# Moving the block turns and the loads of y to GpSimd's queue, lowering the rank of the square transposes, and pairing two output blocks of each down projection

## The chip, the cores and the metric

The kernel runs on one core of a Trainium2 chip. The metric is the device time of one execution in microseconds. The kernel before takes 2028.07 us (median of 3 runs, 2026.43 to 2028.74). The profile comes from one more execution, which took 2025.24 us.

## The reference, cut to what matters

One layer of a streaming encoder is computed for 384 rows: 256 prompt frames of one stream, and 16 new frames of each of 8 running streams. All data are float32.

```python
h    = rmsnorm(x, norm_mix_g)
proj = h @ w_in                                   # GLU halves, q, k, v, forget logits, gates A and B
u    = glu_in[..., :D_CONV] * sigmoid(glu_in[..., D_CONV:])
z    = layernorm(causal_dwconv(ext, conv_dw_w, conv_dw_b), conv_ln_g, conv_ln_b)
a_out = (z * sigmoid(z)) @ conv_pw_out
b_out = attn_fn(q, k, v, logf) @ w_att_out
x    = x + (gate_a * a_out + gate_b * b_out) @ w_out
h2   = rmsnorm(x, norm_ffn_g)
up   = h2 @ w_up                                  # gate half g and value half u, 5632 columns each
gc   = causal_dwconv(ext_f, ffn_dw_w, ffn_dw_b)   # 3 taps on the gate half
x    = x + (silu(gc) * u_half) @ w_down
```

`D_MODEL` is 2048, `D_FF` 5632. The change touches the last three products: `conv_pw_out`, `w_out`, and the up and down projections.

## The kernel before, in words

**Rows and splitting.** The 384 rows are three tiles of 128 (`NTT = 3`). Every product is made from split operands: each is kept as `hi`, a copy in the type fp32r, and `lo`, what the copy leaves over, and each product of two 128-row blocks takes three matmuls (L233 to L235): hi by hi, hi by lo, lo by hi. The activations are split once. The weights are streamed: `fetch` (L129, queue of SyncE) loads 512 KB, two contraction blocks of 128 by 512 columns, into one of three `raw` buffers. `split` makes `hi` on ScalarE (L138, two buffers) and `lo` on VectorE (L139, two buffers). One such chunk feeds 18 matmuls of 512 columns (2 contraction blocks, 3 row tiles, 3 matmuls).

**Jobs.** `gemm` takes a list of jobs. A job is one 512-column output block: `nk` contraction steps, three PSUM banks `acc` (one for each row tile; the pool has 5 banks), then `evac` for each bank and `done`. Jobs in a tuple share their steps: chunk by chunk the first job's two steps, then the second's; its third bank comes from the pool `misc`. Before the change only the first two jobs of v are paired. `plan` lists the weight chunks in the order in which jobs take them.

**Turning.** A product's output has rows on partitions, but the next product needs it with columns on partitions. The class `Turned` does this for blocks of 128 by 512 for each of three row tiles. First, `swap` transposes 32x32 squares on VectorE (L247). Second, `quadrants_out` (L253) writes the squares to DRAM with four DMAs of 192 KB (`turn<-block`). Third, `quadrants_in` (L259) reads them back in the turned order with one DMA of 768 KB (`block<-turn`), which waits for all four. There are 30 such turns: four in the `conv_pw_out` stage (`pw_job`, giving `mix`), four in the `w_out` stage (`wo_job`, giving `xg`), and 22 in the up projections (a gate half and a value half for each of 11 groups). One more, of the state of the FFN convolution (`sft`), is written out beside them.

**What follows a turn.** For `mix`, ScalarE copies the turned block to `hi` (L882) and VectorE makes `lo` (L883). For `xg`, it is L931 to L933. For a gate half, ScalarE copies into `extf` (L978), GpSimd fills the borders (L981 to L985), VectorE does the taps (L997, L999). For a value half, VectorE multiplies (L1013), ScalarE and VectorE split (L1017, L1018) into `act`. The FFN runs in the order of `FFN_PLAN`: up groups 0 to 4, down over groups 0 to 3, up 5 to 8, down over 4 to 7, up 9 and 10, down over 8 to 10. Each down projection has four jobs, one for each 512 output columns, and adds into `y` (L1039).

**Order.** TensorE's order is written out by hand. On the other engines a scheduler fixes one order for each engine when the program is built; an instruction with a higher rank goes first among those that it holds ready. The rank is the place in the program, moved forward inside `tc.high_priority(offset=...)`: 150 places for fetch and split, 60 for `evac`, 400 for the turn's DMAs. On the chip each engine and each DMA queue then keeps to that order: an instruction that waits holds up all behind it. All of the weight loads, turn DMAs and loads of `y` (L907) are in SyncE's queue.

**The two stages with most of the changed work.** In `pw_job`, `ev` does on VectorE, at the rank of `evac`, for each row tile: gate times bank (L872), add of the other branch (L873), and the swap (L247). In `wo_job` it is the add to `y` (L919) and the swap. In `up_jobs`, ScalarE moves the bank to `rows` (L1030), and VectorE swaps.

Of the kernel before, what the change touches and what calls it, by code (L numbers as in the profile page):

```python
# [11 lines left out]
ALU = mybir.AluOpType  # L12
# [3 lines left out]
P = 128  # L16
DM = 2048
NT = 384
NTT = 3
# [10 lines left out]
CONV_START = 56  # L30
CONV_RATE = ((CONV_START, 0.0), (176, 1.3), (240, 0.6), (1 << 20, 1.4))
LN_LAG = 4
SPLIT_AHEAD, EVAC_AHEAD, MOVE_AHEAD = 150, 60, 400

R_FFN, R_DWB, R_LNG, R_LNB, R_FDB, R_QG, R_N = 0, 16, 24, 32, 40, 84, 85
WARM, WARM_MID, WARM_END = 6, 2, 4
# [3 lines left out]
def hybrid_step(  # L40
# [9 lines left out]
    nc = tc.nc  # L50
# [23 lines left out]
    def f(ap):  # L74
        return ap.bitcast(F32)
# [3 lines left out]
    tt = nc.vector.tensor_tensor  # L79
# [6 lines left out]
    xin = [x_prompt[0, 0:P, :], x_prompt[0, P:2 * P, :], x_sample.rearrange("b t d -> (b t) d")]  # L86
# [57 lines left out]
    def planned(w, k0, cols, nk, *more):  # L144
        for k in range(k0, k0 + nk, 2):
            for cl in (cols,) + more:
                plan.append([w[0, k * P:(k + 2) * P, c:c + n].rearrange("(k p) n -> p k n", p=P) for c, n in cl])

    def up_cols(g):
        return [[(512 * g, 512)], [(DFF + 512 * g, 512)]]  # L150
# [7 lines left out]
    N_COLS = [[(512 * g, 512)] for g in range(4)]  # L158
# [13 lines left out]
    for what, g in FFN_PLAN:  # L172
        if what == "up":
            for cols in up_cols(g):
                planned(w_up, 0, cols, 16)
        else:
            for cols in N_COLS:
                planned(w_down, 4 * g[0], cols, 4 * len(g))

    v_last = len(plan) - 16  # L180
# [4 lines left out]
    def after(units, fn):  # L185
        later.append([units, fn])
# [8 lines left out]
    def grouped(tiles):  # L195
        def get(k):
            t = tiles[k // 4]
            return t[:, 0, k % 4, :], t[:, 1, k % 4, :]
        return get
# [46 lines left out]
    def swap_blocks(dst, src, q):  # L246
        nc.vector.transpose(dst.rearrange("p i q c -> p q i c"), src.rearrange("p (q i c) -> p q i c", q=q, i=4))  # L247

    def quadrants_out(src, n):
        d = p_dr.tile([4, 32, 4, n], F32, tag="turn", bufs=4, name="turn")  # L250
        with tc.high_priority(offset=MOVE_AHEAD):
            for i in range(4):
                nc.sync.dma_start(d[:, :, i, :].rearrange("j r n -> r j n"),  # L253
                                  src[32 * i:32 * i + 32, :].rearrange("r (j n) -> r j n", j=4))
        return d

    def quadrants_in(dst, d):
        with tc.high_priority(offset=MOVE_AHEAD):
            nc.sync.dma_start(dst, d[:].rearrange("j r i n -> (j r) (i n)"))  # L259

    class Turned:
        def __init__(self, block, rows):
# [1 line left out]
            w = self.work[:].rearrange("p (i t q c) -> p i t q c", i=4, t=NTT, c=32)  # L264
            self.w = [w[:, :, t] for t in range(NTT)]

        def swap(self, t):
            swap_blocks(self.w[t], self.rows[:, t, :], 4)

        def moved(self):  # L270
            out = self.block()
            quadrants_in(out[:], quadrants_out(self.work[:], 384))
            return out[:].rearrange("p (i t q c) -> p i t q c", i=4, t=NTT, q=4)

    def natural(ap):
        return ap.rearrange("p (t i c) -> p i t c", t=NTT, i=4)
# [5 lines left out]
    def job(kind, nk, act, evac, n=512, done=None):  # L282
        d = dict(kind=kind, nk=nk, act=act, evac=evac, n=n)
        if done is not None:
            d["done"] = done
        return d
# [61 lines left out]
    def panels(name):  # L348
        return [p_sg.tile([P, NTT, 512], F32, tag=f"S{n}", name=f"{name}{n}") for n in range(4)]
# [208 lines left out]
    def tiny(name):  # L558
        return p_qkv.tile([P, NTT, H], F32, name=name)

    z, e, r, s2, pl = tiny("lz"), tiny("le"), tiny("lr"), tiny("ls"), tiny("lpoly")
# [212 lines left out]
    sgA = panels("sgA")  # L774
# [20 lines left out]
    sgB = [p_z.tile([P, NTT, 512], F32, name=f"sgB{n}") for n in range(4)]  # L795
# [69 lines left out]
    def pw_job(g):  # L865
        box = []

        def ev(t, ps):
            if t == 0:
                box.append(Turned(mix_block, sgA[g]))  # L870
            a, b = sgA[g][:, t, :], sgB[g][:, t, :]
            tt(a, ps[:], a, op=ALU.mult)  # L872
            tt(a, a, b, op=ALU.add)  # L873
            box[0].swap(t)

        def done():
            d = box[0].moved()

            def parts(m):
                v = d[:, :, :, m, :]  # L880
                hi, lo = natural(mix[g][:, 0, m, :]), natural(mix[g][:, 1, m, :])
                nc.scalar.copy(hi, v)  # L882
                tt(lo, v, f(hi), op=ALU.subtract)  # L883
            for m in range(4):
                after(3 + m // 2, lambda m=m: parts(m))
        return job("B", 8, grouped(zt), ev, done=done)
# [14 lines left out]
    y = []  # L901

    def load_y():
        y.extend(panels("y"))
        for n in range(4):
            for t in range(NTT):
                nc.sync.dma_start(y[n][:, t, :], xin[t][:, n * 512:(n + 1) * 512])  # L907

    def block():
        return p_w.tile([P, NTT * 512], F32, tag="block", bufs=4, name="block")  # L910

    def wo_job(n):
        box = []

        def ev(t, ps):
            ys = y[n][:, t, :]
            if t == 0:
                box.append(Turned(block, y[n]))
            tt(ys, ps[:], ys, op=ALU.add)  # L919
            box[0].swap(t)  # L920
            jk = p_w.tile([P, 512], F32, tag="jk", bufs=1, name="jk2")
            nc.scalar.activation(jk[:], ys, AF.Square, accum_out=ss2[:, t, n:n + 1])

        def done():
            d = box[0].moved()

            def parts(m):
                v = d[:, :, :, m, :]
                g = col[:, R_FFN + 4 * n + m:R_FFN + 4 * n + m + 1]
                hi, lo = natural(xg[n][:, 0, m, :]), natural(xg[n][:, 1, m, :])  # L930
                nc.scalar.activation(v, v, AF.Identity, scale=g)  # L931
                nc.scalar.copy(hi, v)
                tt(lo, v, f(hi), op=ALU.subtract)  # L933
            for m in range(4):
                after(3 + m // 2, lambda m=m: parts(m))
            if n == 3:
                second_norm()
        return job("B", 16, grouped(mix), ev, done=done)

    def second_norm():  # L940
        m2 = p_w.tile([P, NTT], F32, name="m2")
        nc.vector.tensor_reduce(m2[:], ss2[:], axis=mybir.AxisListType.X, op=ALU.add)
        ts(m2[:], m2[:], 1.0 / DM, EPS, op0=ALU.mult, op1=ALU.add)
        newton_rsqrt(r2[:], p_w.tile([P, NTT], F32, name="r2s")[:], m2[:])

    after(8, load_y)
    gemm([wo_job(n) for n in range(4)])
    p_f, close_f = pool("ffn")
# [5 lines left out]
    for i in range(4):  # L954
        nc.sync.dma_start(sr[32 * i:32 * i + 16, :], sf_rows[:, 1408 * i:1408 * (i + 1)])
    swap_blocks(sw.rearrange("p (i q c) -> p i q c", i=4, c=32), sr, 11)
    quadrants_in(sft[:].rearrange("p a c -> p (a c)"), quadrants_out(sw, 352))

    extf = [p_f.tile([P, 24, 18], F32, name=f"extf{m}") for m in range(4)]
# [62 lines left out]
    def up_jobs(g):  # L1022
        def half(finish):
            box = []

            def ev(t, ps):
                if t == 0:
                    rows = block()[:].rearrange("p (t n) -> p t n", t=NTT)
                    box.append(Turned(block, rows))
                nc.scalar.activation(box[0].rows[:, t, :], ps[:], AF.Identity, scale=r2[:, t:t + 1])  # L1030
                box[0].swap(t)
            return job("B", 16, xa, ev, done=finish(g, box))
        return [half(up_g_done), half(up_u_done)]

    def down_jobs(gs, last):
        def evac(n):
            def ev(t, ps):
                ys = y[n][:, t, :]
                tt(ys, ps[:], ys, op=ALU.add)  # L1039
                if last:  # L1040
                    dst = [y_prompt[0, 0:P], y_prompt[0, P:2 * P], y_sample.rearrange("b t d -> (b t) d")][t]
                    nc.sync.dma_start(dst[:, n * 512:(n + 1) * 512], ys)
            return ev

        def act(k):
            return grouped([acts[g] for g in gs])(k)

        return [job("B", 4 * len(gs), act, evac(n)) for n in range(4)]

    for what, g in FFN_PLAN:  # L1050
        gemm(up_jobs(g) if what == "up" else down_jobs(g, g[-1] == 10))
# [45 lines left out]
```

## Time and profile before

| | |
|---|---|
| runs | 2028.07 us median (2026.43 to 2028.74) |
| profiled execution | 2025.24 us, of which 2023.5 us is the span from the first to the last instruction |
| granted TensorE clock over the span | 0.997 |
| VectorE busy | 1054.6 us (52%) |
| ScalarE busy | 772.5 us (38%) |
| GpSimd busy | 96.7 us (5%) |
| DMA | 324.63 MB, mean 160 GB/s; the queue of SyncE's DMAs 52.2% of 16 engines' span |

The page gives busy times, the busy share in 40 slices, the chain that ended last, and groups of instructions. In rows of the timeline the first number is the start in us from the beginning of the span, the second the length, then engine, line, operation and tiles; in brackets stands the engine's idle time just before and what ended it. An engine name with a q (SPq) is a queue's issue of a DMA, not the transfer. Matmuls overlap, so their starts, not their lengths, give the pace.

### The profile page before, as it was taken

Reading aid. Unit: us, or ns where it says so; the run is one execution under the profiler, and the core shown is the slowest. Engines: PE = TensorE matmul, PEld = TensorE weight load, DVE = VectorE, ACT = ScalarE, POOL = GpSimd, SP = SyncE. Lnnn points to the kernel's source line nnn. Section 1 sums busy time; section 2 is a strip of 40 time slices with the busy share of each in tenths; the row PEclk is TensorE's granted clock in tenths of the full one; section 3 lists DMA queues with packets and bytes.
Section 4 is the critical chain, followed back from the end, with each engine's and each line's share of the span. In section 5 each row is a group of like instructions: output and inputs, shape, how many; then the busy total and the mean of one; then the engine's idle time right before and its main releaser. Section 6 shows DMA issues by size and latency. Waiting matters only on the chain.

```text
span 2023.5 us, 24649 instructions
## 1 busy us (share of the span) xinstructions
PE 2004.1 (99%) x9498; PEld 1689.0 (83%) x9498; DVE 1054.6 (52%) x1459; ACT 772.5 (38%) x1148; POOL 96.7 (5%) x251
## 2 busy tenths in 40 slices
PE   9999999999999998999999999999999999999999
PEld 9999888888888886888888888888888888888877
DVE  4477868547466346454545545433445554334543
ACT  5433344555325332344434334222333332223422
POOL 1000100000000000000100111000100110001000
PEclk9999999999999999999999999999999999999999
DMA  6444645554344446756655565544555554446543
GB/s 187 133 133 113 201 144 167 171 161 141 115 127 125 127 144 194 243 168 190 198 178 179 176 189 160 163 132 128 172 183 172 177 182 138 133 126 193 166 162 125
DMA packets 197340, 324.63 MB, mean 160 GB/s; under 512 B 14542, under 2 KB 80585, under 8 KB 197215
## 3 DMA queue, kind: packets, MB, share of 16 engines
q1 hardware_dynamic: 196615, 322.35, 52.2%
q8 instruction: 74, 1.21, 0.3%
q0 software_dynamic: 288, 0.57, 0.2%
q14 instruction: 43, 0.35, 0.1%
q10 hardware_dynamic: 320, 0.14, 0.0%
HBM read 291.30 MB, written 32.17 MB: 160 GB/s over the span
## 4 chain that ended last, share of the span: by engine, by line
PE 97%; DVE 1%; DMA 1%; ACT 0%; issue 0%; SPq 0%; ACTq 0%; DVEq 0%
PE acc L234 29%; PE acc L233 29%; PE acc L235 29%; PE acc L230 2%; PE acc L228 2%; PE acc L229 2%; DVE lo L139 0%; DMA raw<-in_w_up_dram 0%; PE misc L673 0%; PE misc L299 0%; DVE sgA L872 0%; PE misc L739 0%; PE misc L706 0%; ACT hi L138 0%; DMA turn<-block 0%
## 5 line engine op out<-in xcount | busy, mean ns | idle before, releaser
L139 DVE TENSOR_TENSOR lo<-raw,hi 128x1024 fp32r<-128x1024 f32 (+2 forms) x481 | 579.4, 1205 | 842.0 <-ACT hi L138 837.6
L138 ACT CAST hi<-raw 128x1024 fp32r<-128x1024 f32 (+2 forms) x481 | 498.3, 1036 | 1080.1 <-PE acc L235 955.7
L234 PE MATMUL acc<-lo,xg 128*128 128x512 f32 x1056 | 410.9, 389 | 0.7 <-DVE lo L139 0.7
L233 PE MATMUL acc<-hi,xg 128*128 128x512 f32 x1056 | 410.8, 389 | 0.0
L235 PE MATMUL acc<-hi,xg 128*128 128x512 f32 x1056 | 410.8, 389 | 0.0
L233 PE MATMUL acc<-hi,hT 128*128 128x512 f32 (+1 forms) x704 | 272.1, 386 | 0.1
L234 PE MATMUL acc<-lo,hT 128*128 128x512 f32 (+1 forms) x704 | 265.7, 377 | 0.3 <-DVE lo L139 0.3
L235 PE MATMUL acc<-hi,hT 128*128 128x512 f32 (+1 forms) x704 | 265.7, 377 | 0.0
L234 PEld LDWEIGHTS acc<-lo,xg 128*128 128x128 f32 x1056 | 198.2, 188 | 42.3 <-DVE lo L139 1.1
L233 PEld LDWEIGHTS acc<-hi,xg 128*128 128x128 f32 x1056 | 198.2, 188 | 41.2
L235 PEld LDWEIGHTS acc<-hi,xg 128*128 128x128 f32 x1056 | 198.2, 188 | 41.0
L233 PE MATMUL acc<-hi,act 128*128 128x512 f32 x528 | 206.2, 391 | 3.4 <-ACT act L1017 3.4
L234 PE MATMUL acc<-lo,act 128*128 128x512 f32 x528 | 206.1, 390 | 0.0
L235 PE MATMUL acc<-hi,act 128*128 128x512 f32 x528 | 206.0, 390 | 0.0
L502 DVE SCALAR_TENSOR_TENSOR ut<-ext,cw,ut 128x384 f32<-128x384 f32 x240 | 150.0, 625 | 5.9
L233 PEld LDWEIGHTS acc<-hi,hT 128*128 128x128 f32 x704 | 132.2, 188 | 23.7 <-issue 1.8
L235 PEld LDWEIGHTS acc<-hi,hT 128*128 128x128 f32 x704 | 132.1, 188 | 23.3
L234 PEld LDWEIGHTS acc<-lo,hT 128*128 128x128 f32 x704 | 132.4, 188 | 22.3 <-DVE lo L139 1.6
L233 PEld LDWEIGHTS acc<-hi,act 128*128 128x128 f32 x528 | 99.4, 188 | 24.6 <-ACT act L1017 3.8
L235 PEld LDWEIGHTS acc<-hi,act 128*128 128x128 f32 x528 | 99.5, 188 | 20.9 <-DVE act L1018 0.3
L234 PEld LDWEIGHTS acc<-lo,act 128*128 128x128 f32 x528 | 99.5, 188 | 20.7
L228 PE MATMUL acc<-hT,hi 128*128 128x384 f32 x256 | 86.0, 336 | 0.1
(289 smaller groups left out, 1943.2 us busy)
## 6 DMA issues: line engine op xcount, KB each, us to landing
raw<-in_w_up_dram SPq DMA_DIRECT2D x176, 512.0 KB
raw<-in_w_in_dram SPq DMA_DIRECT2D x96, 512.0 KB
raw<-in_w_down_dram SPq DMA_DIRECT2D x88, 512.0 KB
turn<-block SPq DMA_DIRECT2D x120, 192.0 KB
block<-turn SPq DMA_DIRECT2D x30, 768.0 KB
raw<-in_w_in_dram SPq DMA_DIRECT2D x64, 256.0 KB
raw<-in_w_out_dram SPq DMA_DIRECT2D x32, 512.0 KB
raw<-in_w_att_out_dram SPq DMA_DIRECT2D x16, 512.0 KB
```

Of the source, the lines that this page charges most:

```text
L138: nc.scalar.copy(hi[:, k, :o], raw[:, k, :o])
L139: tt(lo[:, k, :o], raw[:, k, :o], f(hi[:, k, :o]), op=ALU.subtract)
L228: mm(o, hi[:, kk, s], ah, start=st, stop=False)
L229: mm(o, hi[:, kk, s], al, start=False, stop=False)
L230: mm(o, lo[:, kk, s], ah, start=False, stop=sp)
L233: mm(o, ah[:, s], hi[:, kk, :n], start=st, stop=False)
L234: mm(o, ah[:, s], lo[:, kk, :n], start=False, stop=False)
L235: mm(o, al[:, s], hi[:, kk, :n], start=False, stop=sp)
L502: stt(o, v, wc, o, op0=ALU.mult, op1=ALU.add)
```

## The change

1. The four DMAs out and the one DMA in of each turn, including the turn of the FFN state, go from SyncE's queue to GpSimd's, at the ordinary rank.
2. The swaps go out of `ev` into `moved`, which `done` calls: they come after all three banks are evacuated and have the ordinary rank. In `pw_job` the add of the other branch (L873) moves into `done` too.
3. The loads of `y` are issued by GpSimd, the two prompt tiles of a block in one DMA: 8 DMAs instead of 12, of the same 3 MB.
4. In each down projection the first two jobs are a tuple, and the plan of weight chunks alternates between them.

```diff
-SPLIT_AHEAD, EVAC_AHEAD, MOVE_AHEAD = 150, 60, 400
+SPLIT_AHEAD, EVAC_AHEAD = 150, 60
...
-            for cols in N_COLS:
+            planned(w_down, 4 * g[0], N_COLS[0], 4 * len(g), N_COLS[1])
+            for cols in N_COLS[2:]:
                 planned(w_down, 4 * g[0], cols, 4 * len(g))
...
     def quadrants_out(src, n):
         d = p_dr.tile([4, 32, 4, n], F32, tag="turn", bufs=4, name="turn")
-        with tc.high_priority(offset=MOVE_AHEAD):
-            for i in range(4):
-                nc.sync.dma_start(d[:, :, i, :].rearrange("j r n -> r j n"),
-                                  src[32 * i:32 * i + 32, :].rearrange("r (j n) -> r j n", j=4))
+        for i in range(4):
+            nc.gpsimd.dma_start(d[:, :, i, :].rearrange("j r n -> r j n"),
+                                src[32 * i:32 * i + 32, :].rearrange("r (j n) -> r j n", j=4))
         return d
 
     def quadrants_in(dst, d):
-        with tc.high_priority(offset=MOVE_AHEAD):
-            nc.sync.dma_start(dst, d[:].rearrange("j r i n -> (j r) (i n)"))
+        nc.gpsimd.dma_start(dst, d[:].rearrange("j r i n -> (j r) (i n)"))
...
-        def swap(self, t):
-            swap_blocks(self.w[t], self.rows[:, t, :], 4)
-
         def moved(self):
+            for t in range(NTT):
+                swap_blocks(self.w[t], self.rows[:, t, :], 4)
             out = self.block()
...
-            a, b = sgA[g][:, t, :], sgB[g][:, t, :]
+            a = sgA[g][:, t, :]
             tt(a, ps[:], a, op=ALU.mult)
-            tt(a, a, b, op=ALU.add)
-            box[0].swap(t)
 
         def done():
+            for t in range(NTT):
+                a, b = sgA[g][:, t, :], sgB[g][:, t, :]
+                tt(a, a, b, op=ALU.add)
             d = box[0].moved()
...
-            for t in range(NTT):
-                nc.sync.dma_start(y[n][:, t, :], xin[t][:, n * 512:(n + 1) * 512])
+            cs = slice(512 * n, 512 * (n + 1))
+            nc.gpsimd.dma_start(y[n][:, 0:2, :], x_prompt[0, :, cs].rearrange("(t p) d -> p t d", p=P))
+            nc.gpsimd.dma_start(y[n][:, 2, :], xin[2][:, cs])
...
-            box[0].swap(t)
             jk = p_w.tile([P, 512], F32, tag="jk", bufs=1, name="jk2")
...
-                box[0].swap(t)
             return job("B", 16, xa, ev, done=finish(g, box))
...
-        return [job("B", 4 * len(gs), act, evac(n)) for n in range(4)]
+        jobs = [job("B", 4 * len(gs), act, evac(n)) for n in range(4)]
+        return [(jobs[0], jobs[1])] + jobs[2:]
```

## The prediction

> **What bounds the kernel now.** I read the page first, then who waits for whom on PE, then PE's timeline at each of those waits, then VectorE, ScalarE and the DMA queues around them.
>
> ```profile
> span 2023.5 us, 24649 instructions
> PE 2004.1 (99%) x9498; PEld 1689.0 (83%) x9498; DVE 1054.6 (52%) x1459; ACT 772.5 (38%) x1148; POOL 96.7 (5%) x251
> ```
>
> PE is busy in all but 19.4 us. The change removes no matmul, so it can only win back idle time of PE, or add to it. The waits:
>
> ```profile
> PE acc L234 <- DVE lo L139: 7.9, 5, 4.0
> PE acc L233 <- ACT act L1017: 3.4, 1, 3.4
> ```
>
> The rest of that view is start-up and a few tenths. On PE's timeline these waits are five idles in the stages that the change touches (a sixth row, 800.86, marks the start of the first `w_out` job):
>
> ```profile
> 766.45 0.50 PE L234 MATMUL acc<-lo,zt 128*128 128x512 f32 x1 [0.65 <-DVE lo L139]
> 783.02 0.50 PE L234 MATMUL acc<-lo,zt 128*128 128x512 f32 x1 [4.00 <-DVE lo L139]
> 800.86 0.39 PE L233 MATMUL acc<-hi,mix 128*128 128x512 f32 x1
> 803.46 0.50 PE L234 MATMUL acc<-lo,mix 128*128 128x512 f32 x1 [2.21 <-DVE lo L139]
> 985.64 0.50 PE L234 MATMUL acc<-lo,xg 128*128 128x512 f32 x1 [0.73 <-DVE lo L139]
> 1935.64 0.50 PE L233 MATMUL acc<-hi,act 128*128 128x512 f32 x1 [3.40 <-ACT act L1017]
> ```
>
> They sum to 10.99 us. The longer ones cost more than the idle. In the windows view (length, then busy us and instructions of PE, PEld, DVE, ACT, POOL, then granted clock, DMA share, GB/s):
>
> ```profile
> 780.00:789.00 9.00, 5.98 (x19) 4.81 (x20) 7.18 (x12) 1.72 (x5) 0.00 (x0) 0.81 0.47 132
> 801.00:810.00 9.00, 6.79 (x24) 5.20 (x23) 7.49 (x12) 3.44 (x6) 0.00 (x0) 0.81 0.55 178
> 983.00:987.00 4.00, 3.27 (x15) 2.41 (x14) 2.43 (x2) 2.71 (x4) 0.03 (x1) 1.00 0.96 342
> 1931.00:1942.00 11.00, 7.60 (x26) 5.59 (x25) 5.16 (x9) 3.15 (x6) 0.00 (x0) 0.84 0.36 126
> ```
>
> After idles of 2.21 us and more the granted clock falls: 0.19 x 9.00 = 1.7 us lost twice, and 0.16 x 11.00 = 1.8 us; after 0.73 us it stays at 1.00. So the five places hold 11.0 + 5.2 = 16.2 us in all. That is the most that the change can win here, about 0.8%.
>
> **The change, part by part.**
>
> *Pairing in the down projections.* The idle at 1935.64 is the last down projection reaching group 10 too early:
>
> ```profile
> 1934.50 1.02 DVE L1013 TENSOR_TENSOR ac<-block,gc 128x384 f32<-128x384 f32 x2
> 1935.08 0.98 ACT L1017 CAST act<-ac 128x384 fp32r<-128x384 f32 x2 [1.76 <-DVE ac L1013]
> ```
>
> Steps 0 to 7 of the job use groups 8 and 9, and step 8 needs group 10. A chunk of two steps takes 4.08 us (the spacing of the `lo` rows below), so step 8 comes 16.3 us after the start. With two jobs in alternation it comes after 32.6 us: need moves 16.3 us later, the wait was 3.4 us. All of it goes, with its 1.8 us of clock: -5.2 us. It costs nothing: matmuls, chunks and banks are the same in number; the pair takes the 5 `acc` banks and one `misc` bank that the FFN never used, and the first job's banks are evacuated during the second's last 4.08 us. If that cover were gone, three adds of 0.7 us (as L872 below) would show.
>
> *The `conv_pw_out` stage.* Before the 4.00 us idle VectorE had this order:
>
> ```profile
> 777.48 1.37 DVE L872 TENSOR_TENSOR sgA<-acc,sgA 128x512 f32<-128x512 f32 x2 [4.49 <-PE acc L235]
> 778.77 1.28 DVE L873 TENSOR_TENSOR sgA<-sgA,sgB 128x512 f32<-128x512 f32 x2
> 779.97 0.68 DVE L872 TENSOR_TENSOR sgA<-acc,sgA 128x512 f32<-128x512 f32 x1
> 780.57 1.29 DVE L247 STREAM_TRANSPOSE block<-sgA 128x512 f32<-128x512 f32 x2
> 781.79 1.18 DVE L139 TENSOR_TENSOR lo<-raw,hi 128x1024 fp32r<-128x1024 f32 x1
> ```
>
> The `hi` that this `lo` needs was made here, itself after a wait for its weights:
>
> ```profile
> 775.98 1.05 ACT L138 CAST hi<-raw 128x1024 fp32r<-128x1024 f32 x1 [4.25 <-DMA raw<-in_conv_pw_out_dram]
> ```
>
> So `lo` could have begun at 777.03 and began at 781.79: 4.8 us behind evacuation, adds and swaps, whose place ahead of it had been fixed at the build. And the weights came late because of the queue:
>
> ```profile
> 767.05 2.07 SPq L253 DMA_DIRECT2D turn<-block  x4
> 769.22 1.59 SPq L129 DMA_DIRECT2D raw<-in_conv_pw_out_dram  x2
> ```
>
> The next `raw` stands behind four turn DMAs, which wait for the last swap and take 2.07 us to issue. The change takes both away: weights no longer stand behind a turn, and three adds and three swaps, 3 x 0.64 + 3 x 0.65 = 3.9 us, lose their rank. The same work remains, with VectorE free before and after. The three idles (0.65, 4.00, 2.21) and 3.4 us of clock go: -10.3 us. This is the least certain term, since the order is made anew at the build: between 0 (the rival below) and -10.3 I take the whole, since the row at 781.79 shows both causes and the change removes both.
>
> *The first up projection.* From the chain of waits:
>
> ```profile
> 969.57 3.90 DMA turn<-block
> 975.54 7.63 DMA raw<-in_w_up_dram
> ```
>
> SyncE's queue waited 3.90 us for the state's turn, with weights behind it. On GpSimd's queue that wait holds up only the next turn. The 0.73 us go; bounds 0 and -0.73, for the transfers still share the engines (342 GB/s in that window).
>
> *What GpSimd's queue costs.* The nearest rows (line, engine, min/median/max ns; then KB and us from issue to landing):
>
> ```profile
> L362 POOL DMA_DIRECT2D kg<-in_k_norm_g_dram x1 | 0.6, 569 | 0.0
> L797 POOL DMA_DIRECT2D out_dram<-in_state_conv_dram x1: 523/523/523, 371.2 to 371.2; - x1
> ```
>
> ```profile
> out_dram<-in_state_conv_dram POOLq DMA_DIRECT2D x1, 448.0 KB, 4.6
> vrow<-in_norm_ffn_g_dram POOLq DMA_DIRECT2D x1, 8.0 KB, 2.9
> vrow<-in_conv_ln_b_dram POOLq DMA_DIRECT2D x1, 4.0 KB, 4.7
> ```
>
> A turn there is 4 x 0.52 + landing 2.9 to 4.7 + 0.57 + landing 4.6 to 7.9 (4.6 scaled by 768/448, an estimate): 10.2 to 15.3 us. In the FFN SyncE's turn gives this, from the last swap to the product:
>
> ```profile
> 1069.81 0.70 DVE L247 STREAM_TRANSPOSE block<-block 128x512 f32<-128x512 f32 x1
> 1084.73 1.23 DVE L139 TENSOR_TENSOR lo<-raw,hi 128x1024 fp32r<-128x1024 f32 x1 [2.85 <-ACT hi L138]
> 1085.87 1.02 DVE L1013 TENSOR_TENSOR ac<-block,gc 128x384 f32<-128x384 f32 x2
> 1088.81 1.23 DVE L139 TENSOR_TENSOR lo<-raw,hi 128x1024 fp32r<-128x1024 f32 x1 [1.92 <-ACT hi L138]
> ```
>
> That is 1085.87 - 1070.51 = 15.4 us, so the upper bound just fits. A later landing holds up the next `lo` only after 1.92 us, and PE only after a further 4.08 - 1.05 - 1.23 = 1.8 us: from a turn of 19.1 us on. I take 0 for the 22 FFN turns. GpSimd's in-order queue holds the `extf` copies behind them, which need the turn anyway.
>
> *What is late next.* The last `mix` block is needed at step 12 of the first `w_out` job, 6 chunks after 800.86: at 825.3.
>
> ```profile
> 807.78 0.70 DVE L247 STREAM_TRANSPOSE block<-sgA 128x512 f32<-128x512 f32 x1
> 827.82 1.96 DVE L883 TENSOR_TENSOR mix<-block,mix 128x384 fp32r<-128x384 f32 x4
> ```
>
> Today it is first ready at 827.82 + 0.49 = 828.3, and does not stall only because the idle and slow clock at 803.46 (2.2 + 1.7) put the need at 829.2. Without them it is 3.0 us late. From the last swap at 808.48 GpSimd's turn would land at 818.7 to 823.8, early enough, but ScalarE takes the block between two splits 4.08 us apart. I give back half of that, 2.0 us, and half of a clock loss, 0.9 us: +2.9 us; bounds 0 and 5.8.
>
> *The loads of y* cost PE nothing: first needed after the first `w_out` job; what they can hold up is a rival.
>
> Sum: -5.2 - 10.3 - 0.7 + 2.9 = -13.3 us. The profiled execution's 2025.24 us would become 2011.9; it lay 2.8 us under the median of the runs, so against 2028.07 I predict 2014.8 us. With the bounds of the last term and 2 us left of the stage's idles this case runs from 2011.5 to 2020.
>
> **The rivals.**
>
> *The weights stay late (20%).* Turns and weights still share the transfer capacity, and a new fixed order may again put `lo` behind VectorE's other work. For it: the stage's VectorE work per job stays the same. Against it: the 2.07 us of issue do leave the queue. Only the pairing and the first up projection count: -5.9 us, 2022.2. [...] The window at 983 agrees that the transfers share (0.96 busy).
>
> *The loads of y block the last mix turn (10%).* All 3.1 MB can now be issued in a few us, with the last `block<-turn` behind them in the same queue: at 342 GB/s, 9 us. It would land at up to 833, 8 us late, plus clock 1.7: gain 16.2 - 9.7 = 6.5, 2021.6. Before, two of the twelve loads, of 256 KB each, went out ahead of that turn:
>
> ```profile
> 804.99 0.94 SPq L907 DMA_DIRECT2D y<-in_x_prompt_dram  x2
> ```
>
> *GpSimd's issues wait for VectorE (13%, the slower side).* If each of a turn's five issues waits out a VectorE instruction of up to 1.23 us, the turn grows by 6.2 us: up to 21.5, which is 2.4 beyond the 19.1 at which the value half decides. In 11 value halves that is 26 us, with 13.3 saved: +13, 2041. Against it stands this row, beside the issue at 371.2:
>
> ```profile
> 371.15 1.22 DVE L139 TENSOR_TENSOR lo<-raw,hi 128x1024 fp32r<-128x1024 f32 x1
> ```
>
> Neither took longer than usual (523 ns, 1.22 us), but it is one issue, of another shape. [...]
>
> *Waits only move (7%).* Each idle removed comes back elsewhere, within 4 us of 2028.
>
> **How the numbers follow.** Forecast 50%, rivals 20, 10, 13 and 7. A measurement can tell about 0.2%, 4 us. The forecast and the first two rivals are faster, less 3% of the first rival that ends within 4 us: faster 0.77. Same 0.10, slower 0.13. The range 2011.5 to 2026 holds the first three cases and their bounds, and leaves out the slower case and most of the last.
>
> **What would show it.** Right: no `act` wait at the last down projection; no PE idle over 1 us between 740 and 805; weights issued within 0.5 us after the `lo` that frees their buffer; GpSimd's issues near 0.55 us. Wrong: VectorE's L1013 or ScalarE's L978 idle on a turn in the FFN; a new idle of PE on `mix` at step 12; `lo` still behind L873 and L247.

## The result, and the profile after

| | before | after |
|---|---|---|
| median of the runs | 2027.33 us (4 runs, 2026.43 to 2028.74) | 2009.37 us (4 runs, 2008.51 to 2009.47) |
| ratio | | 0.991, 95% interval 0.9893 to 0.9927 |
| profiled execution, and its span | 2025.24 us, 2023.5 us | 2009.28 us, 2007.3 us |
| granted clock over the span | 0.997 | 1.0 |

The kernel is 18.0 us faster. The forecast was 2014.8 us, with a range that began at 2011.5: the direction is right, the gain is 4.7 us larger than the 13.3 us forecast, and the time lies below the range. The page of the kernel after:

```profile
span 2007.3 us, 24719 instructions
PE 1999.1 (100%) x9498; PEld 1687.7 (84%) x9498; DVE 1051.0 (52%) x1459; ACT 777.6 (39%) x1148; POOL 182.0 (9%) x414
```

PE is now idle for 8.2 us of the span instead of 19.4. Who waits for whom on PE, in the kernel after (us in total, times, longest):

```profile
PE misc L316 <- POOL ident masks.py:199: 2.5, 1, 2.5
PE misc L486 <- ACT kTs L672: 0.5, 1, 0.5
PE acc L231 <- DVE lo L139: 0.4, 1, 0.4
PE acc L235 <- DVE lo L139: 0.3, 1, 0.3
```

The wait for `act` (3.4 us) is gone, and the two waits for `lo` that are left are under half a microsecond each and lie in the first 61 us, outside the changed stages; the kernel before has both as well. What stays is the start. The same four windows that the prediction shows (length, busy us of PE, PEld, DVE, ACT, POOL, granted clock, DMA share, GB/s):

```profile
780.00:789.00 9.00, 9.00 (x41) 7.47 (x40) 8.09 (x13) 3.76 (x6) 3.48 (x6) 1.00 0.72 219
801.00:810.00 9.00, 9.00 (x41) 7.44 (x41) 4.91 (x7) 3.02 (x5) 4.14 (x8) 1.00 0.75 251
983.00:987.00 4.00, 4.00 (x19) 3.30 (x19) 2.68 (x5) 2.63 (x6) 2.67 (x10) 1.00 0.45 124
1931.00:1942.00 11.00, 11.00 (x50) 9.13 (x49) 3.58 (x3) 2.11 (x2) 0.00 (x0) 1.00 0.34 110
```

PE is busy throughout, at clock 1.00. The profiled executions differ by 16.0 us, and the prediction had counted 16.2 us of idle and slow clock in these places: nearly all of it was won, and nothing was given back.

Where the 4.00 us idle was, VectorE's order in the kernel after is this:

```profile
775.81 1.23 DVE L139 TENSOR_TENSOR lo<-raw,hi 128x1024 fp32r<-128x1024 f32 x1 [2.85 <-ACT hi L138]
777.44 1.37 DVE L870 TENSOR_TENSOR sgA<-acc,sgA 128x512 f32<-128x512 f32 x2 [0.41 <-PE acc L236]
778.73 0.68 DVE L875 TENSOR_TENSOR sgA<-sgA,sgB 128x512 f32<-128x512 f32 x1
779.33 0.68 DVE L870 TENSOR_TENSOR sgA<-acc,sgA 128x512 f32<-128x512 f32 x1
779.93 1.22 DVE L139 TENSOR_TENSOR lo<-raw,hi 128x1024 fp32r<-128x1024 f32 x1
```

The first `lo` is that of the next job's first chunk. It now stands ahead of the evacuation, not behind it and the adds and swaps. In ScalarE's row for its `hi`, PE and no longer a DMA ended the wait:

```profile
774.72 1.05 ACT L138 CAST hi<-raw 128x1024 fp32r<-128x1024 f32 x1 [3.02 <-PE acc L236]
```

SyncE's queue holds nothing but weights from 740 to 863 us, and GpSimd's holds the turns (issue time in ns, least, median and most; then the first and the last start in us):

```profile
740.34 37.09 SPq L129 DMA_DIRECT2D raw<-in_conv_pw_out_dram  x10
781.17 81.98 SPq L129 DMA_DIRECT2D raw<-in_w_out_dram  x21
```

```profile
L253 POOL DMA_DIRECT2D turn<-block x124: 550/551/601, 751.8 to 1910.2; - x124
L258 POOL DMA_DIRECT2D block<-turn x30: 547/556/561, 759.5 to 1915.1; - x30
```

With the one DMA in of the state's turn (556 ns) these are 155 issues, and all took 547 to 601 ns. At most 50 ns over the median, none waited out an instruction of VectorE such as the `lo` of 1.23 us.

### The profile page after: what moved, and what is told of

Its sections match the earlier page's. It is cut to its first block, busy times and chain, and to the rows that moved or that the text cites. A ratio compares the mean times of both kernels' runs of the same rounds, so it can differ in the third digit from the quotient of the medians.

```text
span 2007.3 us, 24719 instructions
## 1 busy us (share of the span) xinstructions
PE 1999.1 (100%) x9498; PEld 1687.7 (84%) x9498; DVE 1051.0 (52%) x1459; ACT 777.6 (39%) x1148; POOL 182.0 (9%) x414
## 4 chain that ended last, share of the span: by engine, by line
PE 99%; DVE 1%; issue 0%; POOL 0%; ACT 0%; POOLq 0%; DVEq 0%
PE acc L234 29%; PE acc L235 29%; PE acc L236 29%; PE acc L231 2%; PE acc L230 2%; PE acc L229 2%; PE misc L234 1%; PE misc L235 1%; PE misc L236 1%; PE misc L671 0%; PE misc L297 0%; PE misc L737 0%; PE misc L704 0%; DVE lo L139 0%; DVE gc L998 0%
## 5 line engine op out<-in xcount | busy, mean ns | idle before, releaser
L234 PE MATMUL acc<-hi,act 128*128 128x512 f32 x484 | 188.3, 389 | 0.0
L235 PE MATMUL acc<-lo,act 128*128 128x512 f32 x484 | 188.3, 389 | 0.0
L236 PE MATMUL acc<-hi,act 128*128 128x512 f32 x484 | 188.3, 389 | 0.0
L253 POOL DMA_DIRECT2D turn<-block x124 | 67.9, 554 | 927.5 <-DVE block L248 902.4
L234 PEld LDWEIGHTS acc<-hi,act 128*128 128x128 f32 x484 | 90.9, 188 | 18.9
L235 PEld LDWEIGHTS acc<-lo,act 128*128 128x128 f32 x484 | 90.9, 188 | 18.9
L236 PEld LDWEIGHTS acc<-hi,act 128*128 128x128 f32 x484 | 90.9, 188 | 18.7
```

The lines of the kernel that those rows point to most:

```text
L234: mm(o, ah[:, s], hi[:, kk, :n], start=st, stop=False)
L235: mm(o, ah[:, s], lo[:, kk, :n], start=False, stop=False)
L236: mm(o, al[:, s], hi[:, kk, :n], start=False, stop=sp)
L253: nc.gpsimd.dma_start(d[:, :, i, :].rearrange("j r n -> r j n"), src[32 * i:32 * i + 32, :].rearrange("r (j n) -> r j n", j=4))
```

## The experiments

Each kernel was compared with runs of the kernel before on the same chip, whose medians lay between 2026.04 and 2027.06 us from chip to chip.

### The four parts, one at a time

Each of these is the kernel before with one part of the change: `pair_only` has part 4, `queue_only` the turns of part 1, `rank_only` part 2, `y_only` part 3. In `queue_only` the turns' DMAs also lose their high rank, as in the change; no run moves the queue and keeps that rank.

> Only the pairing of the first two jobs of each down projection; everything else as before. Both theories: the 3.4 us wait for act at the last down projection and its 1.8 us of clock go, the four other idles of PE stay. About -5.2 us, ratio 0.9974. Were the pairing without effect or costly in banks, the ratio would be 1.000 or above.

> Only the turns' DMAs go to GpSimd's queue; the swaps and adds keep the rank of the evacuation, the loads of y stay in SyncE's queue, nothing is paired. Queue theory: the weights' place behind the turns is the root of the late lo, in fact and in the order fixed at the build; the three idles of the conv_pw_out stage (10.3 us with clock) and the 0.7 us of the first up projection go, the act wait of 5.2 us stays: about -11 us, ratio 0.9946. Rank theory: the adds and swaps still stand ahead of lo, most of the 10.3 us stays: -1 to -4 us, ratio 0.998 to 0.9995.

> Only the swaps and the adds of the other branch move behind the evacuation, at the ordinary rank; the turns stay in SyncE's queue at their high rank. Rank theory: lo is no longer behind adds and swaps, the three idles go: about -10 us, ratio 0.995. Queue theory: the weights are still late behind the turns, so lo is still placed late; 0 to -4 us, ratio 0.998 to 1.000, and possibly slower, since the turn begins later.

> Only the loads of y go to GpSimd's queue. Both theories: PE waits for nothing that they hold up, so no difference, ratio 0.999 to 1.001. If the loads of y in SyncE's queue cost the weights time at the start of the w_out stage, the 2.21 us idle and its 1.7 us of clock shrink: down to 0.998.

| kernel | median us (runs) | ratio to before, 95% interval | gain us |
|---|---|---|---|
| before | 2026.23 (25) | | |
| pair_only | 2021.08 (9) | 0.9976 (0.9966 to 0.9986) | 5.2 |
| queue_only | 2013.92 (5) | 0.9941 (0.9929 to 0.9954) | 12.3 |
| rank_only | 2026.19 (11) | 1.0003 (0.9994 to 1.0012) | 0 |
| y_only | 2026.45 (11) | 1.0001 (0.9992 to 1.0009) | 0 |

The queue and the pairing make up the whole: 12.3 + 5.2 = 17.5 of 18.0 us. PE's waits for `lo` in `pair_only`, then in `rank_only`, and the only wait of over 0.6 us that `queue_only` has left after the start-up:

```profile
PE acc L235 <- DVE lo L139: 7.7, 5, 4.0
```

```profile
PE acc L234 <- DVE lo L139: 7.8, 5, 4.0
```

```profile
PE acc L233 <- ACT act L1015: 3.4, 1, 3.4
```

Four of the five waits for `lo` are the idles of 0.65, 4.00, 2.21 and 0.73 us; the fifth, of 0.3 us, lies at 9 us. Lowering the rank of adds and swaps leaves the four as they were (0.53, 4.01, 2.21 and 0.76 us). Moving the turns to another queue, with adds and swaps at their old rank, removes all four. The opposite cut agrees. `no_rank` is the kernel after without part 2:

```diff
         def moved(self):
-            for t in range(NTT):
-                swap_blocks(self.w[t], self.rows[:, t, :], 4)
...
+            tt(a, a, b, op=ALU.add)
+            box[0].swap(t)
```

> The kernel after, with adds and swaps back in ev at the rank of evac. Queue theory (the three idles came from turns in SyncE's queue alone, and rank_only's ratio of 1.0003 shows that rank is worth nothing): as after, 2009 to 2010.5, no idle of PE over 0.7 us from 740 to 805. Theory of the prediction (VectorE's order was a cause of its own): the 4.00 us idle comes back in part, 2011 to 2016.

It took 2009.21 us (5 runs; ratio 0.9914, 0.9901 to 0.9928), as the kernel after. The rank of adds and swaps is worth nothing that these runs can show, alone or with the rest.

### How the queue does it: order_only

A queue can act in two ways: weights arrive late on the chip, or the scheduler, which knows of the queue, fixes a worse order. `order_only` keeps the kernel before, with all turns in SyncE's queue, and forces VectorE's order (`behind` adds a constraint of order without a wait). So that there is a second `lo` to stand behind, `ahead(2)` also takes the next chunk's fetch and split earlier.

```diff
+                    if j.get("split_first"):    # conv_pw_out jobs only
+                        ahead(2)
...
-            tt(a, ps[:], a, op=ALU.mult)
-            tt(a, a, b, op=ALU.add)
-            box[0].swap(t)
+            behind(tt(a, ps[:], a, op=ALU.mult), los[-2])
+            behind(tt(a, a, b, op=ALU.add), los[-1])
+            behind(box[0].swap(t), los[-1])
```

> The kernel before (turns still in SyncE's queue), with VectorE's order in the conv_pw_out stage forced at the build: evacuation, adds and swaps come behind the lo of the chunks that TensorE needs next. Two ways in which the queue can have made the 4.00 us idle: (a) through the order: sharing the queue made the scheduler place lo late, and the weights themselves were early enough (hi at 775.98 + 1.05, lo could end at 778.2, the idle ends at 783.0). Then the idles of 0.65, 4.00 and 2.21 us go with this edit: about -10 us, ratio 0.995, and with queue_only's share (12.3 us) little is left for the queue on the chip. (b) through real lateness on the chip: weights behind the turn's DMAs in the queue. Then the idles stay or move: 2024 to 2028, ratio 0.999 to 1.001.

It took 2015.21 us (5 runs) against 2026.93: 11.7 us faster, ratio 0.9943 (0.993 to 0.9955). Its timeline at the same place (SPq is SyncE's queue):

```profile
764.00 0.37 SPq L129 DMA_DIRECT2D raw<-in_conv_pw_out_dram  x1
768.75 2.07 SPq L261 DMA_DIRECT2D turn<-block  x4
770.92 1.63 SPq L129 DMA_DIRECT2D raw<-in_conv_pw_out_dram  x2
...
773.90 1.06 ACT L138 CAST hi<-raw 128x1024 fp32r<-128x1024 f32 x1 [1.36 <-PE acc L241]
...
774.99 1.22 DVE L139 TENSOR_TENSOR lo<-raw,hi 128x1024 fp32r<-128x1024 f32 x1 [0.98 <-ACT hi L138]
776.62 2.05 DVE L880 TENSOR_TENSOR sgA<-acc,sgA 128x512 f32<-128x512 f32 x3 [0.41 <-PE acc L241]
```

With `lo` ahead of the evacuation the three idles of the stage are gone, and `hi` waits for PE, no longer for its weights. But the edit changes SyncE's order too. The weights of this `hi` were issued at 764.00, ahead of the turn; in the kernel before, those of the same chunk went out at 769.22, behind it. So this run alone doesn't tell the order on VectorE from late weights. The kernel before does, for two of its three idles. The `hi` copies that feed the `lo` of 765.21 (idle of 0.65 us) and of 802.19 (2.21 us) had their weights in time and waited for PE:

```profile
761.53 1.06 ACT L138 CAST hi<-raw 128x1024 fp32r<-128x1024 f32 x1 [3.02 <-PE acc L235]
...
796.98 1.05 ACT L138 CAST hi<-raw 128x1024 fp32r<-128x1024 f32 x1 [3.02 <-PE acc L235]
```

At the idle of 4.00 us the weights were late, but not late enough: `hi` was done at 777.03, so `lo` could have been done at 778.2, and PE needed it at 779.0. `order_back0` below makes such idles with every weight in time. Together these say that the queue acted through the order fixed at the build. Why the scheduler placed `lo` there, presumably because it reckoned the weights late behind the turn, is argued and not shown. `order_pair` adds the pairing to `order_only`.

> order_only with the pairing of the down projections: turns, swaps' rank and loads of y as before, all in SyncE's queue. If the order of VectorE at the build and the early act of group 10 are the whole cost, it is as the kernel after but for the 0.7 us of the first up projection: 2015.2 - 5.1 = 2010.1, ratio 0.9915 to 0.9925. If the new queue of the turns has a gain of its own on the chip, it stays at 2012 or more.

2010.09 us (5 runs, ratio 0.9919, 0.9906 to 0.9933): the whole gain, less 0.7 us, with every DMA still in its old queue. PE's idle of 0.76 us at the first up projection stays in it (0.70 in `order_only`) and is gone in `queue_only`: that one goes with the queue, not with the order forced here.

### Which lo counts: order_back and order_back0

These two put a late `lo` back into the kernel `no_rank`, whose weights are early and alone in their queue. `order_back` holds the next `lo` to be traced behind the second swap, `order_back0` also traces the first chunk's split after the evacuation, so that it is that one.

```diff
+            if ahead_of_lo:                       # in split
+                behind(i, ahead_of_lo.pop())
...
+            if t == 1:                            # in ev of pw_job
+                ahead_of_lo.append(s)
...
-                    ahead(2)                      # order_back0 only
+                    ahead(1 if j.get("split_late") and k == nk - 2 else 2)
```

> no_rank (2009.21 us: the kernel after, adds and swaps in ev), with one order forced at the build: the lo of each job's second chunk comes behind two of the swaps of the job before, as in the kernel before; turns stay in GpSimd's queue, weights alone in SyncE's. Order theory: this alone brings the idles back at the four job ends of the conv_pw_out stage, lo done some 4.3 + 1.2 us after evacuation began, so 2 to 4 us of idle and 0 to 1.8 us of clock each: +8 to +22, 2017 to 2031. If a late lo costs only together with weights behind turns: under 4 us, 2009 to 2013.

This missed: 2009.16 us (4 runs, ratio 0.9917, 0.9904 to 0.9931). The forced `lo` was the second chunk's:

```profile
780.79 1.18 DVE L139 TENSOR_TENSOR lo<-raw,hi 128x1024 fp32r<-128x1024 f32 x1
```

The stage's jobs end at 778.44 there, so the second chunk's `lo` is needed at about 782.7; it is done at 781.97. Adds and swaps ahead of it cost nothing.

> order_back held up the lo of the wrong chunk: the second, which TensorE needs a whole chunk (4.08 us) after the job's end. Here it is the lo of the next job's first chunk that is put behind two of the swaps, in the kernel after with adds and swaps in ev; turns stay in GpSimd's queue, so weights are early. Order theory: TensorE needs that lo some 0.2 us after the job's last matmul, which is 1.4 us after evacuation began; behind two evacuations, two adds and two swaps it is done 4.9 us after evacuation began: 3.3 us of idle at each of the four job ends and 0 to 1.8 us of clock each: +13 to +20, 2022 to 2030. If a late lo costs only together with weights behind turns on the chip: under 4 us, 2009 to 2013.

2032.10 us (11 runs, ratio 1.0026, 1.0017 to 1.0035): 22.9 us slower than `no_rank`, with every weight in time. One job end, with the `hi` of that `lo` and VectorE's order, and PE at all four:

```profile
761.67 1.06 ACT L138 CAST hi<-raw 128x1024 fp32r<-128x1024 f32 x1 [3.02 <-PE acc L244]
...
764.39 1.37 DVE L879 TENSOR_TENSOR sgA<-acc,sgA 128x512 f32<-128x512 f32 x2 [4.49 <-PE acc L244]
...
768.10 2.32 DVE L139 TENSOR_TENSOR lo<-raw,hi 128x1024 fp32r<-128x1024 f32 x2
```

```profile
749.33 0.50 PE L243 MATMUL acc<-lo,zt 128*128 128x512 f32 x1 [3.40 <-DVE lo L139]
...
769.34 0.80 PE L243 MATMUL acc<-lo,zt 128*128 128x512 f32 x1 [3.40 <-DVE lo L139]
...
791.92 0.79 PE L243 MATMUL acc<-lo,zt 128*128 128x512 f32 x1 [3.40 <-DVE lo L139]
...
813.48 0.79 PE L243 MATMUL acc<-lo,mix 128*128 128x512 f32 x1 [3.40 <-DVE lo L139]
```

The 4.49 us for which VectorE stands idle ahead of the evacuation is the same number as in the kernel before (777.48). The order of that one `lo` is enough to make the idles. In the kernel before the idles of 4.00 and 2.21 us followed such a first `lo`; that of 0.65 us followed the second chunk's, which was done 6.2 us after evacuation began (760.17 to 766.40). The windows behind the four idles:

```profile
749.00:758.00 9.00, 8.67 (x38) 7.21 (x39) 4.64 (x6) 1.47 (x2) 3.56 (x6) 1.00 0.71 210
769.00:778.00 9.00, 8.66 (x27) 6.91 (x28) 5.93 (x10) 1.55 (x3) 3.50 (x6) 0.68 0.72 207
791.00:800.00 9.00, 8.08 (x29) 6.57 (x30) 6.90 (x10) 1.09 (x2) 3.49 (x6) 0.81 0.63 189
813.00:822.00 9.00, 8.52 (x26) 6.78 (x27) 5.83 (x10) 1.05 (x1) 3.49 (x6) 0.66 0.60 181
```

Four idles of the same 3.40 us are followed by a granted clock of 1.00, 0.68, 0.81 and 0.66 over 9 us: 0, 2.9, 1.7 and 3.1 us lost. Idle and clock, 13.6 and 7.7 us, come to about the 21.2 us by which the profiled execution (2030.39) is slower than that of `no_rank`. The expected 2022 to 2030 allowed at most 1.8 us of clock for each idle.

### Longer turns, and another queue: slow3, act_queue, y_burst

`slow3` adds three dummy DMAs of 768 KB to each turn, in GpSimd's queue.

```diff
-            quadrants_in(out[:], quadrants_out(self.work[:], 384))
+            d = quadrants_out(self.work[:], 384)
+            for _ in range(3):
+                spare = p_dr.tile([P, 1536], F32, tag="spare", bufs=4, name="spare")
+                nc.gpsimd.dma_start(spare[:], self.work[:])
+            quadrants_in(out[:], d)
```

> The kernel after, with three more DMAs of 768 KB (the turn's work block, to a spare DRAM tile) in GpSimd's queue between the four out and the one in of each of the 30 turns: extra work whose results nothing reads. Each at 2.3 us by 342 GB/s makes a turn some 7 to 12 us longer, so 15.6 becomes 23 to 28 us, beyond the 19.1 us from which the prediction says that a value half's product decides. Frozen order (the prediction's working): 11 value halves wait 4 to 9 us each, 40 to 100 us with the clock, 2050 to 2110. Rival: the order is made anew at the build with the longer turn in it, so other work stands ahead of the product, and only places with a deadline pay (the last mix block at step 12 of the first w_out job, the last xg block, the first down job of each group): under 20 us, 2010 to 2030.

2032.49 us (7 runs, ratio 1.0026, 1.0016 to 1.0037), 23.1 us over the kernel after: a little above the rival's bound, far below the frozen order's. PE's waits:

```profile
PE acc L234 <- ACT mix L885: 8.9, 2, 5.6
PE acc L234 <- ACT xg L935: 2.6, 1, 2.6
```

No wait is for `act`. From the last swap to the value half's product it took 18.4 to 20.9 us (15.6 in the kernel after), and PE did not notice: the product stands later in the new order. The bill comes in the `conv_pw_out` and `w_out` stages, above all at the `mix` blocks. In ten of the 11 groups the dummies made this stretch 3 to 4 us longer, not 7 to 12; a turn's DMA in landed 9.7 us after its issue at the median, against 5.7 in the kernel after.

`act_queue` is the kernel after with `nc.scalar.dma_start` for `nc.gpsimd.dma_start` in the turns.

> The kernel after, with the turns' DMAs issued by ScalarE instead of GpSimd. Any queue but SyncE's does (the gain is only that weights no longer stand behind a turn): 2009 to 2011. It must be an engine with nothing urgent behind the turn: ScalarE makes each chunk's hi (1.05 us every 4.08 us) in the same in-order stream, and a turn's DMA in waits some 3 us for the four out to land, with hi behind it; if the order fixed at the build puts hi behind such a wait, PE idles in up to 30 turns, at 1 to 3 us each with the clock: 2030 to 2090.

2018.88 us (4 runs, ratio 0.9963, 0.9949 to 0.9976): neither case as stated. `hi` stood behind a turn's wait at four places, 11.3 us in all, and PE lost 0.77 us by it, at one of them (972.59); what it pays for is a turn behind `hi`. The last `mix` turn (first DMA out, and the copy):

```profile
803.24 0.31 ACTq L253 DMA_DIRECT2D turn<-block  x1
...
824.74 1.76 ACT L881 CAST mix<-block 128x384 fp32r<-128x384 f32 x4 [4.21 <-DMA block<-turn]
```

Its four DMAs out left one `hi` apart, from 803.24 to 815.41, and the copy of the block began 21.5 us after the first. PE idles 5.86 us for it, by far its longest wait.

`y_burst` forces all eight loads of `y` behind the last turn's four DMAs out and its DMA in behind them (`behind` again, on GpSimd's queue).

> The kernel after, with all eight loads of y (3.1 MB) forced between the four out and the one in of the last mix turn, as the second rival has it. Rival's working: 9 us later at 342 GB/s; the last mix block is needed at 819.5 and its product of ScalarE begins at 816.5 now, so with little slack PE idles 4 to 9 us there, plus 1.7 to 3 us of clock: 2015 to 2021. If the loads only wait behind the turn on the 16 engines or the block has slack: 2009 to 2011.

2016.67 us (4 runs, ratio 0.9954, 0.9941 to 0.9968), 7.3 us over the kernel after, as the rival had it:

```profile
811.04 0.55 POOL L264 DMA_DIRECT2D block<-turn  x1 [2.87 <-DMA y<-in_x_prompt_dram]
...
824.08 0.79 PE L234 MATMUL acc<-hi,mix 128*128 128x512 f32 x1 [5.22 <-ACT mix L901]
```

### The term that failed: swap_twice and swap_four

In the kernel after, the last `mix` turn ran like this (first `w_out` matmul, last swaps, ScalarE's copy):

```profile
794.92 0.39 PE L234 MATMUL acc<-hi,mix 128*128 128x512 f32 x1
...
798.59 1.89 DVE L248 STREAM_TRANSPOSE block<-sgA 128x512 f32<-128x512 f32 x3
...
816.47 1.75 ACT L881 CAST mix<-block 128x384 fp32r<-128x384 f32 x4
```

The block is needed 24.5 us after the first row, at 819.4; the trace has it landed at 815.4. The last swap ends at 800.48, 5.6 us after the first row; the prediction had left it at 7.6 us (808.48 against 800.86). Two kernels move it later by doing swaps of the last turn again:

```diff
-            for t in range(NTT):
+            for t in list(range(NTT)) * times:              # swap_twice, times = 2 for g == 3
+            for t in list(range(NTT)) + [0] * (times - 1):  # swap_four
```

> The kernel after, with the three swaps of the last mix turn done twice (the same values again), so that the last one ends some 2 us later, 7.2 us after the end of the stage: what the prediction assumed (808.48 with the stage's end at 800.86, 7.6 us). The prediction's working: the block is then late for step 12 of the first w_out job, 2.0 us of idle (0 to 4) and 0.9 of clock: 2012.3, between 2009.4 and 2015.2. Rival: the turn on GpSimd's queue is short enough (12.2 to 15.2 us from the last swap to landing) and ScalarE's place for the block moves with it: no idle on mix, 2009 to 2010.

2013.91 us (4 runs, ratio 0.9937, 0.9922 to 0.9952). The last swap ended at 806.00, 11.5 us after the first `w_out` matmul (794.52) and later than meant, and ScalarE waited for the block:

```profile
821.35 1.75 ACT L881 CAST mix<-block 128x384 fp32r<-128x384 f32 x4 [1.11 <-DMA block<-turn]
```

That is past the point in question, so it does not tell the two apart.

> The kernel after, with one of the three swaps of the last mix turn done once more, behind the others. In swap_twice the last swap ended 11.5 us after the first w_out matmul (806.00 against 794.52), not 7.2 as meant, since a lo and another block's lo went in between; here I expect 8.5 to 9.2 us, just later than the 7.6 that the prediction assumed. The prediction's working: 2.0 us of idle and 0.9 of clock, 2012.3. From swap_twice (landing 15.35 us after the last swap, TensorE going on 0.57 us after that, need 24.5 us after the first matmul) the last swap may end 8.6 us after it: idle of 0 to 0.6 us, 2009 to 2010.

2012.74 us (4 runs, ratio 0.9932, 0.9915 to 0.9949): 3.4 us over the kernel after, where the prediction's working gives 2.9 and mine from `swap_twice` 0 to 0.6. The last swap ended at 802.97, 9.2 us after the first `w_out` matmul (793.81):

```profile
818.49 1.04 ACT L138 CAST hi<-raw 128x1024 fp32r<-128x1024 f32 x1 [3.02 <-PE acc L236]
819.44 1.75 ACT L881 CAST mix<-block 128x384 fp32r<-128x384 f32 x4
820.00 0.50 PE L234 MATMUL acc<-hi,mix 128*128 128x512 f32 x1 [1.55 <-ACT mix L881]
...
821.31 0.50 PE L236 MATMUL acc<-hi,mix 128*128 128x512 f32 x1 [0.58 <-DVE mix L882]
```

ScalarE did not wait for the block at 819.44 (no idle stands in that row): it was taken behind the split at 818.49, one place too late for step 12. In the trace the block had landed at 817.66, while ScalarE stood idle. The idle is 2.1 us, and the granted clock of 0.81 from 821 to 830 us costs up to 1.7 us. So places 4.08 us apart decide here, not the landing, as the prediction's working has it. Its own 7.6 us is not reached by these two runs, but `order_pair` comes near it from the other side, with the turn in SyncE's queue: its last swap ends at 802.47, 7.3 us after its first `w_out` matmul (795.21), and PE has no idle on `mix`:

```profile
801.77 0.70 DVE L256 STREAM_TRANSPOSE block<-sgA 128x512 f32<-128x512 f32 x1
...
816.77 1.75 ACT L891 CAST mix<-block 128x384 fp32r<-128x384 f32 x4
```

## Why the prediction was wrong, point by point

**The step that failed** is "what is late next": "From the last swap at 808.48 GpSimd's turn would land at 818.7 to 823.8, early enough, but ScalarE takes the block between two splits 4.08 us apart. I give back half of that". Nothing was given back: ScalarE takes the block at 816.47 against a need at 819.4, so the term is 0 where +2.9 us was put down. Such a loss exists, and of that size, when the last swap ends 9.2 us after the first `w_out` matmul (`swap_four`: 2.1 us of idle, 3.4 us in all, against 2.0 and 2.9). The premise failed. The prediction took the need from a stage without idles and the last swap, 7.6 us, from the stage with them; in the kernel after the swap ends at 5.6 us. Even 7.3 us costs nothing in `order_pair`, whose turn is in SyncE's queue. Whether 7.6 us would have cost anything on GpSimd's queue no run shows.

**A second step failed with it: from the profiled execution to the median** the prediction added 2.8 us, the distance of the one from the other in the kernel before. The term above alone would not have left the range: at its own bound of 0 the working still gives 2011.9 us, 2.5 above the measured time. That distance is no constant of the program. Three runs had set the median at 2028.07; 25 later ones set it at 2026.23, 1.0 us above the profiled execution, and spread over 5.1 us (2023.66 to 2028.76). The kernel after spreads over 1.0 us in 4 runs, and its profiled execution lies 0.1 us from its median. The clock goes with the spread: of the 25 runs the three at a granted clock of 0.998 took at most 2024.37 us, the five at 0.995 at least 2026.95. And the clock lost after an idle varies from one time to the next (0 to 3.1 us behind equal idles in `order_back0`). The kernels without the idles spread little (0.4 to 1.0 us in the kernel after, `no_rank` and `order_back`), so the gain between medians is 18.0 us where the profiled executions give 16.0. The variation of the clock is shown; how much of the 2.8 us is clock and how much the small sample or the chip stays open. Without both steps the forecast is 2014.8 - 2.9 - 2.8 = 2009.1 us, which is the profiled execution less the 16.2 us of the five places, against 2009.37 measured.

**Pairing, -5.2 us:** right. `pair_only` gains 5.2 us and loses only the wait for `act`; no add or evacuation shows.

**The conv_pw_out stage, -10.3 us:** right in size, wrong in its reasons. "The row at 781.79 shows both causes and the change removes both": there is one cause, the place of the next job's `lo` on VectorE, the first chunk's at the two longer idles. The queue set it at the build, and the lower rank of adds and swaps, which the prediction counted as a part of the cure, changes nothing (`rank_only`, `no_rank`). The weights' lateness on the chip (4.25 us on a DMA at 775.98) cost nothing by itself: `lo` could still have been done 0.8 us before PE needed it, and at the other two idles the weights were in time. `order_only` gained 11.7 us, 1.4 more than the term, within the spread of the clock in the kernel before.

**The first up projection, -0.7 us:** the idle went with the queue and stays without it, as said. Its time alone is too small to be measured.

**GpSimd's queue, 0 us:** right. From the last swap to the value half's product it is 15.6 us in ten of the 11 groups where SyncE's queue took 15.4. The point of 19.1 us from which it was to decide was worked out in an order that no longer holds once turns get longer: `slow3` goes up to 20.9 us without a wait. Where that point lies in the FFN stays open.

**The rivals.** That weights stay late fell with the profile after. `order_pair` has the whole gain less 0.7 us without another engine: what counted was not the transfers and the 2.07 us of issue, but what a shared queue does to the order fixed at the build. That loads of `y` block the last `mix` turn has the right price (7.3 us in `y_burst`; 9.7 forecast) and does not happen, since each panel of `y` comes free with its own turn: one block goes out between the DMAs out and the DMA in of each of the four turns, not all four blocks at the last. That GpSimd's issues wait for VectorE fell too: 547 to 601 ns for 155 issues, beside a VectorE busy for 52% of the span.

## What to carry to other kernels

Where a scheduler fixes each engine's order at the build, a queue shared by two streams can cost through that order while the transfers themselves are in time (forcing VectorE's order, with every DMA in its old queue, won 11.7 us in `order_only`): compare the order of the engine that ends the wait, and force that order alone before crediting the queue or the rank. When an idle is taken out of a sum, take it out of every time that came after it, the producers' as well as the needs', or the next wait will be forecast from a schedule that no longer exists. And an idle can cost, beyond its length, a clock loss that one profile samples only once (0 to 3.1 us behind the four idles of 3.40 us in `order_back0`), so the distance of a profiled execution from the median must not be carried over to a kernel without the idle.

## What the runs showed of the hardware

Idles of the same 3.40 us at four job ends of one stage, in one execution of `order_back0`, were followed by granted clocks of 1.00, 0.68, 0.81 and 0.66 over the next 9 us. The idle's length does not tell which; what decides it was not tried. The idle of 2.21 us in the kernel before cost 1.7 us of clock too (0.81 granted from 801 to 810 us). GpSimd issued each of a turn's DMAs out in 0.55 us at the median (kernel after), ScalarE in 0.31 us (`act_queue`), and yet ScalarE's queue was the slower place by 9.5 us: the issues of the last `mix` turn each stood behind a `hi`, and PE idled 5.86 us for that block.
